# Filter network with summed last weights, and gate products of a recurrence one tile later

## The chip, the cores and the metric

The kernel runs on one core of a Trainium2 chip. The metric is the device time of one execution in microseconds (us), the median of several. A core has TensorE (PE, matmuls), VectorE (DVE), ScalarE (ACT), GpSimd (POOL) and SyncE (SP, which issues loads); each works off its own queue in order, and they wait for each other by semaphores.

## The reference, cut to what matters

Two blocks of two layers each, 512 tokens, 1024 features, float32. The change touches the mixer of the first block, and the filters of the long convolution of the second block, which are computed there in advance.

```python
# block 1, each layer: a gated linear recurrence beside a latent attention
x_rnn, g_rnn, q_lat, kv_lat, k_rope, gate_a, gate_b = split(x @ w_in)
xc = causal_dwconv(x_rnn, conv_w, conv_b)            # 4 taps
gate_x = sigmoid(blockdiag(xc, gx_w) + gx_b)
gate_a_ = sigmoid(blockdiag(xc, ga_w) + ga_b)
log_a = -8 * gate_a_ * softplus(-lambda)
h_t = exp(log_a)_t * h_{t-1} + (sqrt(1 - exp(2 log_a)) * gate_x * xc)_t
y_rnn = gelu(g_rnn) * h
merged = sigmoid(gate_a) * y_rnn + sigmoid(gate_b) * mla_attention(q_lat, kv_lat, k_rope)
# block 2: filters of the long convolution, both layers
hdn = sin(freq2 * (sin(freq1 * (z @ fw1 + fb1)) @ fw2 + fb2))
filt = hdn @ fw3                                     # [512, 512]: forward, backward
h_fwd, h_bwd = filt[:, :256] * window, filt[:, 256:] * window
k = concatenate([h_fwd, 0, h_bwd[:0:-1]])            # backward row 0 is not used
k = k * rsqrt(sum(k * k) + 1e-6);  kf = rfft(k)
```

## The kernel before

Every float32 product is made of three products of float32r parts (`mm3`): high x high, high x low, low x high. So each weight tile is loaded, cast by ScalarE to its high part (`hiw`, line 336), and VectorE subtracts that to get the low part (`low`, line 337). A stream `W` does this in the order in which weights are used: `get(key)` puts the casts and subtractions of all tiles up to two places behind `key` into the queues of ScalarE and VectorE, at this place of the program. Queues keep the order of the program.

Block 1's mixer makes, for each of eight units m (128 features), four tiles of the input product, x, g, a and b: 24 matmuls of 128 x 512 each. `lru(m)` works on them and hands over (`yield`) at five places; at each of these `tick()` takes the next piece of other work, in layer 0 the filter network and its transforms (`filters`), then the rope tables (`rope_tables`, lines 530 to 560), then the rotated key. In layer 1 there are only the latent queries' norm and the rotated key.

The order in `lru(m)` before: the x tile, the convolution (`xc`, on ScalarE and three VectorE instructions), its split into `xch` and `xcl`; tick; the g tile and its gelu; tick; the gate products `za` and `zx` (three matmuls each), their chain s, r, s, thx on ScalarE (Tanh, Exp, Tanh, Tanh) and v2, s_ on VectorE, a Sqrt; tick; the a tile, its tanh `tha`, GpSimd's product v2 * s_ (VectorE's for the first two units of layer 0), VectorE's scan, gl and ysum; tick; the b tile, its tanh `thb`, and 1 added by GpSimd; tick.

Behind the eight units come the attention's values: eight banks (`vb`, six matmuls each), of which ScalarE casts and VectorE subtracts each half in turn (lines 819, 820); then the key's and queries' products and the first scores (line 965).

`filters` computes the hidden layers, then for each of four time tiles t two products with the layers' last weights (line 1189), multiplies each by the window on VectorE, and makes their sum `sp` and difference `sm` by four GpSimd instructions (lines 1193, 1194); sp and sm are split (`hp`, `hm`) at the next tick, the products squared for the norms, and the squares added up by GpSimd (line 1177). The transforms follow, five ticks for each of four tiles of frequencies, with the weights `dft0` in the stream behind g1 to g4.

Of the kernel before, what the change touches and what calls it, by code (L numbers as in the profile page):

```python
# [13 lines left out]
AF = mybir.ActivationFunctionType  # L14
# [3 lines left out]
DEPTH = 2  # L18
S = 512
D = 1024  # L20
P = 128
# [7 lines left out]
# ------------------------------------------------------------------ layout (host, no arithmetic)  # L29
class Cols:  # L30
    """Per-partition vectors side by side in one [128, n] array."""
# [14 lines left out]
def fold(v):  # L46
    """[n*128] -> [128, n]"""
    return np.asarray(v).reshape(-1, P).T


def mtile(w, cols):
    """stationary tile: the columns of w [K, .] as [128, K/128 * len(cols)]"""
    a = w[:, cols]
    k, m = a.shape
    return a.reshape(k // P, P, m).transpose(1, 0, 2).reshape(P, -1)


def lay_out(i):
    """inputs by name -> DRAM arrays, and the places of the vectors"""
# [67 lines left out]
    # constants of the shapes  # L127
# [11 lines left out]
def lay_out2(g, A, V):  # L139
# [38 lines left out]
    # filter network, both layers side by side  # L178
# [19 lines left out]
    # constants of the shapes  # L198
# [9 lines left out]
    wb = wd.copy()  # L208
    wb[0] = 0.0
    A["wind"] = np.concatenate([wd, wb], axis=1).reshape(4, P, 512)  # L210
# [5 lines left out]
    a = np.stack([C, Sn]).reshape(2, 4, P, 4, P)      # part, tt, t, ft, f  # L216
# [25 lines left out]
    for q in range(8):       # token tile q % 4 of the places: token within the tile, tile  # L242
        io[:, 2 * q:2 * q + 2] = np.stack([r + 1, 0 * r + P * (q % 4)], 1)
    io[:, 16:16 + P] = np.arange(P)
    # tokens of an expert above which it may get a second block with the same weights
# [4 lines left out]
# ------------------------------------------------------------------ kernel  # L250
NE = 18         # blocks of 128 tokens: one of every expert, and a second one of the experts in the last two slots
NS = 3          # experts with slots of their own; the others get theirs by the numbers of their tokens
SLOT = list(range(15)) + [14, 15, 15]       # the slot of a block
XH = 5          # places of two halves for loads, during the experts
AHEAD = 5       # slots that are set ahead of the block at work
XRAW = 2        # places for loads beside those of the weights, during the experts
HOFF = 11       # block from which on loads take no further places
LOOP_PLE = {8: 2}       # quarters of the last gates that come between the experts, by their places
# the order of the pieces of an attention step in block 1
ORDER = "ZQqABSNPKTtM"  # L260
# the pieces of work between the steps of the second attention: keys, queries, spectrum and inverse of the
# long convolution, pooling, gate of the convolution
LP = 3          # piece of the output product behind which the second input of the gates is split
NE2 = 9         # step of the second attention in which the norm of the first head ends
# the order within a step: combine, weights, scores, product with the values, transposes, rest, front
WORK = "cwtpsbf"
# weights whose low parts GpSimd takes
# [5 lines left out]
class Stream:  # L273
    """Weights in the order of their use: DMA, then the exact split into two float32r parts."""

    def __init__(self, k, tag, width, raw, bufs, ahead, pool):
        self.pool = pool
        self.k, self.tag, self.width = k, tag, width
        self.nraw, self.bufs, self.ahead = raw, bufs, ahead
        self.items, self.index = [], {}  # L280
        self.dma_at = self.split_at = 0
        self.fence = None         # no loads from there on
        self.stop = None          # no splits from there on
        self.extra = None         # a pool with XRAW more places for loads
        self.halves = 0           # further places, each of two halves
        self.loads = [0, 0, 0, 0]
        self.spots = []           # tiles that are free for loads
        self.raw, self.parts, self.live = {}, {}, 0
        self.lo_engine = lambda n: "gpsimd" if self.items[n][0][0] in ("uq", "uk") else "vector"
# [57 lines left out]
    def fill(self):  # L347
        """loads into every free place"""
# [29 lines left out]
class Kern:  # L378
# [10 lines left out]
    # tiles  # L389
# [21 lines left out]
    # products  # L411
# [6 lines left out]
    def rms_row(self, sq, n, eps):  # L418
        """1 / sqrt(sum over features / n + eps) of every token, as diagonal blocks; sq: squares [features, tokens];
        eps: a number, or one for every token. rms_spread puts them on all partitions"""  # L420
# [28 lines left out]
    # ---- weights in their order  # L449
# [24 lines left out]
    # ---- constants  # L474
# [19 lines left out]
    def lru_constants(self):  # L494
        """4*softplus(-lambda) and its negative, half biases of the gates: for both layers, [128, 16]"""
# [15 lines left out]
        # log1p(e) = 2 atanh(e / (2 + e)), e = exp(-|lambda|) <= 1  # L511
# [10 lines left out]
        # 2 * (2 acc + max(-lambda, 0))  # L522
# [4 lines left out]
    def rope_tables(self):  # L527
# [29 lines left out]
        # the scale of the scores goes into the queries  # L557
# [3 lines left out]
    # ---- layer norm, one tile of 128 tokens at a time  # L561
    def ln_load(self, row, pool):
        """gain and bias rows, on every partition"""
# [7 lines left out]
    def ln_pre(self, t, gb, eps):  # L571
        """t [128, 1024]: normalised in place"""
# [16 lines left out]
    def ln_post(self, t, xt, x):  # L589
        """token tile t of x, transposed and split into xt = (hi, lo) [128, 8, 512]"""  # L590
# [10 lines left out]
    # ---- out[feature, token] tiles  # L601
# [5 lines left out]
    def start_a(self, keys, xt, between):  # L607
        """the first tiles after a layer norm: the first 256 tokens of all, then the others"""
# [12 lines left out]
    # ---- out[token, feature], 1024 features, accumulated in 8 banks  # L621
# [6 lines left out]
    def gemm_b_ln(self, keys, lhs, banks, first, resid, x, xt, gb, eps, tail=4, after=lambda t: None, late=()):  # L628
        """last part of a product with a layer norm behind it; returns what has to come
        between the first tiles of the next product"""  # L630
        n = len(keys)
        if late:
            # the last bank stays free for the pieces of late
# [10 lines left out]
        for t in range(NT):  # L644
# [4 lines left out]
            if t == NT - 1:  # L649
                # the next weights come before the last norm  # L650
# [9 lines left out]
    # ---- block 1  # L660
    def block1_layer(self, l, xt, x_src):
        """xt: the input, transposed and split; x_src: the same in DRAM. Returns x tiles, xt."""
# [3 lines left out]
        # latent queries, keys; norms over features by a product with ones  # L666
# [80 lines left out]
        # gated linear recurrence  # L747
        ysum, thb = [None] * 8, [None] * 8

        def lru(m):  # L750
# [14 lines left out]
            yield  # L765
            zx, za = self.bank("zx"), self.bank("za")
# [12 lines left out]
            # 1 - r^2 = tanh(-log r) (1 + r^2)  # L779
# [4 lines left out]
            yield  # L784
            ab = tile_of(f"a{m}")
            tha = self.k2(name="tha")
            nc.scalar.activation(tha, ab, AF.Tanh, scale=0.5)
# [5 lines left out]
            yield  # L793
            bb = tile_of(f"b{m}")
            thb[m] = self.k2(name="thb")
            nc.scalar.activation(thb[m], bb, AF.Tanh, scale=0.5)
            nc.gpsimd.tensor_scalar(thb[m], thb[m], 1.0, None, op0=OP.add)
# [8 lines left out]
        # latent attention; the values of even and of odd heads, 128 columns for a head: the high part in the half  # L806
        # of its output rows, the low part in the other one
# [25 lines left out]
        # output product, residual, layer norm  # L833
# [15 lines left out]
        # gated convolution feed-forward  # L849
# [59 lines left out]
    def attention(self, l, ap, kvT, qT, kt, vt, ysum, thb, nope_rows):  # L909
        """16 heads; ysum[m] becomes the (hi, lo) of the merged output of head pair m"""  # L910
# [170 lines left out]
    # ------------------------------------------------------------------ block 2  # L1081
    def plan2(self):
        a, W = self.a, self.W
        for l in range(DEPTH):
# [24 lines left out]
            # in the order of the slots' first blocks; the experts of most slots are set when they are known  # L1109
# [11 lines left out]
    def reduce_angle(self, r, arg, m, ki):  # L1121
        """r = arg - 2 pi k, to be wrapped; m, ki are scratch"""
# [20 lines left out]
    def filters(self, fp):  # L1143
        """the convolution filters of both layers: their spectra go to self.kf, the norms to self.hsc"""
# [11 lines left out]
        wind = [load(a["wind"][t], 512, "wn") for t in range(2)]  # L1156
        h = zT
# [16 lines left out]
        def squares():  # L1174
            """the squares of the last tile join those of the first"""
# [3 lines left out]
        for t in range(4):  # L1179
# [5 lines left out]
            sp, sm = self.k2(name="sp"), self.k2(name="sm")  # L1185
            new = []
            for l in range(DEPTH):
                b = self.bank("filt")
                mm(b, lhsT=h[:, P * t:P * t + P], rhs=f3[l], start=True, stop=True)
                f = self.k2(name="filt")  # L1190
                nc.vector.tensor_tensor(f, b, wn, op=OP.mult)
                c = slice(256 * l, 256 * l + 256)
                nc.gpsimd.tensor_tensor(sp[:, c], f[:, :256], f[:, 256:], op=OP.add)
                nc.gpsimd.tensor_tensor(sm[:, c], f[:, 256:], f[:, :256], op=OP.subtract)
                new.append(f)
            squares()
# [11 lines left out]
        for n in range(4):  # L1208
# [37 lines left out]
            if n == 0:  # L1246
                b = self.bank("hsum")
                for l in range(DEPTH):
                    for c in range(2):
                        for s_ in range(2):  # L1250
                            o = 256 * s_ + P * c
                            mm(b[:, 2 * l + c:2 * l + c + 1], lhsT=fs[l][:, o:o + P], rhs=self.ones[:, 0:1],
                               start=s_ == 0, stop=s_ == 1)
                nc.vector.tensor_scalar(self.hsc, b[:, 0:4], 1e-6, None, op0=OP.add)
# [6 lines left out]
    def constants2(self):  # L1261
        """the loads, and what is left to do once they are there"""
# [21 lines left out]
        def rest():  # L1284
# [10 lines left out]
            for l in range(DEPTH):  # L1295
                li = 0.8 - 0.6 * math.exp(-0.3 * l)
                # its negative
# [967 lines left out]
```

## Time and profile before

| what | value |
|---|---|
| device time, median of 3 runs | 2791.44 us (2790.32 to 2793.89) |
| span of the profiled execution | 2785.1 us; the median lies 6.3 us above it |
| TensorE busy | 2646.0 us, 95% |
| VectorE, ScalarE, GpSimd busy | 65%, 50%, 28% |
| units of layer 0, then layer 1 (from x0 to b7) | about 52 to 289 us; 924 to 1111 us |

Busy time counts an engine's instructions from start to end; overlapping ones are counted once. "Idle before" names the engine whose work ended the wait last. The granted clock is TensorE's: 1.00 is 2.4 GHz, 0.5 would be 1.2 GHz.

### The profile page before, as it was taken

The page shows a single profiled execution, that of the slowest core. Times are in us where ns is not written, and L with a number is a line of the kernel's source. Part 1 is how long each engine was busy: PE and PEld are TensorE (multiplying, and loading weights), DVE is VectorE, ACT ScalarE, POOL GpSimd, SP SyncE. Part 2 cuts the span into 40 slices and gives each one's busy share as a digit, 9 for nine tenths or more (in the row PEclk, how much of TensorE's full clock was granted, in tenths as well). Part 3 has the DMA queues.
Part 4 walks back from the last instruction along what each step waited for, and adds up shares of the span by engine and source line. Part 5 has one row for each costly group of instructions (what it writes and reads, how often), then busy time and mean ns, then how long its engine had stood idle before and what let it go on. Part 6 is the DMA issues. An engine that isn't in the chain of part 4 may idle for free. (4 is left out here: it accounts for less than half of the span.)

```text
span 2785.1 us, 36076 instructions
## 1 busy us (share of the span) xinstructions
PE 2646.0 (95%) x13164; PEld 2188.2 (79%) x13164; DVE 1823.3 (65%) x2685; ACT 1394.4 (50%) x2260; POOL 769.4 (28%) x693
## 2 busy tenths in 40 slices
PE   8899999999999999999999997989999989999996
PEld 6687787888888888778888886867877777778875
DVE  6757686663655555686663657577787656777785
ACT  3666773441442566673442431354287625534782
POOL 1411672000001111771000002354343354624332
PEclk9999999999999999999999998999999999999998
DMA  4233113223232232113233232224598742248974
GB/s 159 89 115 109 57 43 115 83 99 113 91 128 99 72 97 90 48 39 136 76 121 106 91 128 97 70 77 161 213 316 281 215 145 81 90 165 276 342 252 146
DMA packets 120527, 364.17 MB, mean 131 GB/s; under 512 B 18900, under 2 KB 24564, under 8 KB 120344
## 3 DMA queue, kind: packets, MB, share of 16 engines
q1 hardware_dynamic: 100088, 320.14, 33.4%
q0 software_dynamic: 20256, 41.67, 5.6%
q8 instruction: 105, 1.72, 0.3%
q14 instruction: 78, 0.64, 0.1%
HBM read 341.80 MB, written 41.94 MB: 138 GB/s over the span
## 5 line engine op out<-in xcount | busy, mean ns | idle before, releaser
L337 DVE TENSOR_TENSOR low<-raww,hiw 128x1024 fp32r<-128x1024 f32 x350 | 439.0, 1266 | 228.9 <-ACT hiw L336 222.2
L336 ACT CAST hiw<-raww 128x1024 fp32r<-128x1024 f32 (+2 forms) x400 | 409.2, 1036 | 216.4 <-PE acc L416 98.7
L582 POOL TENSOR_TENSOR vare<-bnmv,epsc 128x1 f32<-128x1 f32 x36 | 10.1, 281 | 969.6 <-DVE bnmv L579 969.6
L414 PE MATMUL up<-xt,hiw 128*128 128x512 f32 x704 | 273.9, 389 | 0.0
L415 PE MATMUL up<-xt,hiw 128*128 128x512 f32 x704 | 273.9, 389 | 0.0
L416 PE MATMUL up<-xt,low 128*128 128x512 f32 x704 | 273.9, 389 | 0.0
L877 DVE SCALAR_TENSOR_TENSOR cv<-up,vec,cv 128x510 f32<-128x510 f32 (+1 forms) x176 | 131.9, 749 | 144.5 <-ACT cv L874 141.4
L874 ACT ACTIVATE cv<-up,vec 128x512 f32<-128x512 f32 x88 | 68.7, 781 | 234.2 <-PE up L416 234.2
L414 PEld LDWEIGHTS up<-xt,hiw 128*128 128x128 f32 x704 | 132.1, 188 | 27.5
L416 PEld LDWEIGHTS up<-xt,low 128*128 128x128 f32 x704 | 132.1, 188 | 27.4
L415 PEld LDWEIGHTS up<-xt,hiw 128*128 128x128 f32 x704 | 132.1, 188 | 27.3
L414 PE MATMUL acc<-hiw,h2h 128*128 128x512 f32 x384 | 149.6, 389 | 0.0
L416 PE MATMUL acc<-hiw,h2l 128*128 128x512 f32 x384 | 149.4, 389 | 0.0
L415 PE MATMUL acc<-low,h2h 128*128 128x512 f32 x384 | 149.4, 389 | 0.0
L337 POOL TENSOR_TENSOR low<-raww,hiw 128x1024 fp32r<-128x1024 f32 (+1 forms) x50 | 117.6, 2357 | 38.4 <-ACT hiw L336 24.5
L598 ACT CAST xt<-tp 128x512 fp32r<-128x512 f32 x56 | 29.9, 591 | 186.4 <-PE tp L595 186.1
L1766 POOL DMA_INDIRECT yg<-ye,rt x36 | 57.5, 1598 | 226.1 <-ACT ye L1825 198.7
L414 PE MATMUL g<-hiw,xeh 128*128 128x512 f32 x288 | 118.0, 410 | 1.7 <-ACT xeh L446 1.0
L415 PE MATMUL g<-low,xeh 128*128 128x512 f32 x288 | 117.8, 409 | 1.8 <-DVE low L337 1.4
L416 PE MATMUL g<-hiw,xel 128*128 128x512 f32 x288 | 115.0, 399 | 0.0
L990 POOL TENSOR_SCALAR p<-p,lsum 128x128 f32<-128x128 f32 (+2 forms) x96 | 95.6, 1009 | 36.8 <-DVE lsum L986 36.8
L415 PE MATMUL ga<-xt,hiw 128*128 128x256 f32 x320 | 94.7, 296 | 9.5 <-DVE xt L599 9.3
(611 smaller groups left out, 7699.0 us busy)
## 6 DMA issues: line engine op xcount, KB each, us to landing
raww<-in_w_in_dram SPq DMA_DIRECT2D x108, 512.0 KB
raww<-in_w_up_dram SPq DMA_DIRECT2D x96, 512.0 KB
rawh<-in_w_e_dram SPq DMA_DIRECT2D x108, 256.0 KB
raww<-in_w_e_dram SPq DMA_DIRECT2D x50, 512.0 KB
raww<-in_w_down_dram SPq DMA_DIRECT2D x48, 512.0 KB
x<-in_w_e_dram SPq DMA_DIRECT2D x36, 512.0 KB
rawx<-in_w_e_dram SPq DMA_DIRECT2D x32, 512.0 KB
raww<-in_w_out_dram SPq DMA_DIRECT2D x28, 512.0 KB
```

Source lines behind the costliest of these rows:

```text
L336: nc.scalar.copy(hi[:, c], r)
L337: getattr(nc, self.lo_engine(self.split_at)).tensor_tensor(lo[:, c], r, hi[:, c].bitcast(F32), op=OP.subtract)
L414: mm(out, lhsT=lhs[0], rhs=rhs[0], start=start, stop=False)
L415: mm(out, lhsT=lhs[0], rhs=rhs[1], start=False, stop=False)
L416: mm(out, lhsT=lhs[1], rhs=rhs[0], start=False, stop=stop)
L582: nc.gpsimd.tensor_tensor(ve, mv[:, 1:2], self.eps[:, eps:eps + 1], op=OP.add)
L598: nc.scalar.copy(dst[0], src)
L874: nc.scalar.activation(y, b, AF.Identity, bias=self.v(("fb", l), f), scale=self.v(("fw", l, 2), f))
L877: nc.vector.scalar_tensor_tensor(y[:, d:], b[:, :S - d], self.v(("fw", l, k), f), y[:, d:], op0=OP.mult, op1=OP.add)
L990: eng.tensor_scalar(p[:, c], p[:, c], l_[:, i:i + 1], None, op0=OP.mult)
L1766: nc.gpsimd.indirect_dma_start(out=self.yg, out_offset=bass.IndirectOffsetOnAxis(ap=gi[:, e:e + 1] if row is None else row, axis=0), in_=y ...
```

## The change

The last weights of the filter network are summed and subtracted once (`fsd`, four GpSimd instructions); the products with them give sum and difference of the two directions at once, so the sixteen GpSimd instructions of the time tiles fall away. The window's first row is no longer zero for the backward half, so the first row is mended by three instructions on one partition. The squares are those of sum and difference, and are halved. In `lru` the a tile and its tanh come before the gate products, the b tile and its tanh before v2 * s_ and the scan, and there are four ticks instead of five. Comments and the texts of functions fall away too.

```diff
             gl = self.k2(name="gl")
             nc.scalar.activation(gl, gb, AF.Gelu_apprx_tanh)
             yield
+            ab = tile_of(f"a{m}")
+            tha = self.k2(name="tha")
+            nc.scalar.activation(tha, ab, AF.Tanh, scale=0.5)
+            yield
             zx, za = self.bank("zx"), self.bank("za")
...
             nc.vector.scalar_tensor_tensor(v2, thx, 1.0, xc, op0=OP.add, op1=OP.mult)
-            yield
-            ab = tile_of(f"a{m}")
-            tha = self.k2(name="tha")
-            nc.scalar.activation(tha, ab, AF.Tanh, scale=0.5)
+            bb = tile_of(f"b{m}")
+            thb[m] = self.k2(name="thb")
+            nc.scalar.activation(thb[m], bb, AF.Tanh, scale=0.5)
+            nc.gpsimd.tensor_scalar(thb[m], thb[m], 1.0, None, op0=OP.add)
             (nc.vector if l == 0 and m < 2 else nc.gpsimd).tensor_tensor(v2, v2, s_, op=OP.mult)
             nc.vector.tensor_tensor_scan(thx, r, v2, 0.0, op0=OP.mult, op1=OP.add)
             nc.vector.tensor_tensor(gl, gl, thx, op=OP.mult)
             ysum[m] = self.k2(name="ysum")
             nc.vector.scalar_tensor_tensor(ysum[m], tha, 1.0, gl, op0=OP.add, op1=OP.mult)
             yield
-            bb = tile_of(f"b{m}")
-            thb[m] = self.k2(name="thb")
-            nc.scalar.activation(thb[m], bb, AF.Tanh, scale=0.5)
-            nc.gpsimd.tensor_scalar(thb[m], thb[m], 1.0, None, op0=OP.add)
-            yield
...
         wind = [load(a["wind"][t], 512, "wn") for t in range(2)]
+        fsd = [self.k2(name="fsd") for _ in range(2)]
+        for l in range(DEPTH):
+            for y, op in zip(fsd, (OP.add, OP.subtract)):
+                nc.gpsimd.tensor_tensor(y[:, 256 * l:256 * l + 256], f3[l][:, 256:], f3[l][:, :256], op=op)
...
-            sp, sm = self.k2(name="sp"), self.k2(name="sm")
             new = []
-            for l in range(DEPTH):
+            for w in fsd:
                 b = self.bank("filt")
-                mm(b, lhsT=h[:, P * t:P * t + P], rhs=f3[l], start=True, stop=True)
+                mm(b, lhsT=h[:, P * t:P * t + P], rhs=w, start=True, stop=True)
                 f = self.k2(name="filt")
                 nc.vector.tensor_tensor(f, b, wn, op=OP.mult)
-                c = slice(256 * l, 256 * l + 256)
-                nc.gpsimd.tensor_tensor(sp[:, c], f[:, :256], f[:, 256:], op=OP.add)
-                nc.gpsimd.tensor_tensor(sm[:, c], f[:, 256:], f[:, :256], op=OP.subtract)
                 new.append(f)
+            sp, sm = new
+            if t == 0:
+                nc.vector.tensor_tensor(sm[0:1], sm[0:1], sp[0:1], op=OP.subtract)
+                nc.vector.tensor_scalar(sm[0:1], sm[0:1], 0.5, None, op0=OP.mult)
+                nc.vector.tensor_scalar(sp[0:1], sm[0:1], -1.0, None, op0=OP.mult)
             squares()
...
-                nc.vector.tensor_scalar(self.hsc, b[:, 0:4], 1e-6, None, op0=OP.add)
+                nc.vector.tensor_scalar(self.hsc, b[:, 0:4], 0.5, 1e-6, op0=OP.mult, op1=OP.add)
```

## Rows read from the trace of the kernel before

**Rows 1.** The page: span, and busy time of the engines (share) xinstructions.

```profile
span 2785.1 us, 36076 instructions
...
PE 2646.0 (95%) x13164; PEld 2188.2 (79%) x13164; DVE 1823.3 (65%) x2685; ACT 1394.4 (50%) x2260; POOL 769.4 (28%) x693
```

**Rows 2.** TensorE's waits, 70 to 115 us: total, times, longest.

```profile
PE za L414 <- ACT xch L446: 5.5, 1, 5.5
...
PE in_g L416 <- DVE low L337: 1.7, 1, 1.7
...
PE za L415 <- DVE xcl L447: 0.7, 1, 0.7
```

**Rows 3.** Windows of early layer 0: length, busy by engine, granted clock, DMA.

```profile
66.00:104.60 38.60, 30.93 (x120) 21.77 (x118) 29.35 (x38) 24.33 (x35) 21.54 (x22) 0.99 0.24 75
...
104.60:114.00 9.40, 8.71 (x27) 6.66 (x28) 8.17 (x7) 9.31 (x14) 5.68 (x4) 0.69 0.15 43
```

**Rows 4.** TensorE's waits, 215 to 262 us, and 900 to 1130 us.

```profile
PE in_g L416 <- DVE low L337: 2.2, 1, 2.2
...
PE in_x L416 <- DVE low L337: 0.8, 1, 0.8
```

**Rows 5.** ScalarE's timeline, layer 1, unit 6: start, duration, instruction [idle before].

```profile
1073.92 0.62 ACT L446 CAST xch<-xc 128x512 fp32r<-128x512 f32 x1 [2.44 <-DVE xc L756]
...
1077.61 0.69 ACT L772 ACTIVATE s<-za,hba 128x512 f32<-128x512 f32 x1
...
1086.05 0.60 ACT L787 ACTIVATE tha<-in_a 128x512 f32<-128x512 f32 x1
...
1086.54 1.04 ACT L336 CAST hiw<-raww 128x1024 fp32r<-128x1024 f32 x1
...
1088.38 0.60 ACT L796 ACTIVATE thb<-in_b 128x512 f32<-128x512 f32 x1 [0.80 <-PE in_b L416]
```

**Rows 6.** ScalarE's timeline, layer 1, end of unit 7 and values.

```profile
1111.50 0.60 ACT L796 ACTIVATE thb<-in_b 128x512 f32<-128x512 f32 x1 [1.12 <-PE in_b L416]
...
1116.00 0.88 ACT L819 CAST v<-vb 128x256 fp32r<-128x256 f32 x2 [0.49 <-DVE v L820]
```

**Rows 7.** VectorE's timeline, layer 0, 90 to 97 us.

```profile
90.00 0.68 DVE L447 TENSOR_TENSOR hp<-sp,hp 128x512 fp32r<-128x512 f32 x1
...
95.75 1.81 DVE L447 TENSOR_TENSOR hp<-sp,hp 128x512 fp32r<-128x512 f32 x1 [1.97 <-ACT hp L446]
```

**Rows 8.** TensorE's timeline, layer 0, about 66 us.

```profile
66.00 1.88 PE L1189 MATMUL filt<-f,rad 128*128 128x512 f32 x4
...
67.31 0.79 PE L414 MATMUL za<-xch,hig 128*128 128x512 f32 x1
```

**Rows 9.** GpSimd's timeline, layer 0 at 216 us, layer 1 at 1107 us.

```profile
215.91 1.49 POOL L797 TENSOR_SCALAR thb<-thb 128x512 f32<-128x512 f32 x1 [4.34 <-ACT thb L796]
...
1106.73 1.29 POOL L788 TENSOR_TENSOR v<-v,s 128x512 f32<-128x512 f32 x1 [15.33 <-ACT s L782]
```

**Rows 10.** VectorE's timeline, layer 1, units 6 and 7 and values.

```profile
1071.52 2.32 DVE L756 SCALAR_TENSOR_TENSOR xc<-in_x,vec,xc 128x509 f32<-128x509 f32 x3 [3.02 <-ACT xc L753]
...
1109.03 1.21 DVE L789 TENSOR_TENSOR_SCAN thx<-r,v 128x512 f32<-128x512 f32 x1
...
1111.68 1.22 DVE L337 TENSOR_TENSOR low<-raww,hiw 128x1024 fp32r<-128x1024 f32 x1
...
1114.14 0.42 DVE L820 TENSOR_TENSOR v<-vb,v 128x256 fp32r<-128x256 f32 x1 [1.24 <-ACT v L819]
```

**Rows 11.** Rope tables in layer 0: timelines of ScalarE and of VectorE.

```profile
235.83 1.28 ACT L542 ACT_TABLE_LOAD   x1
...
237.12 0.63 ACT L542 ACTIVATE Sg<-ang 128x512 f32<-128x512 f32 x1
...
253.62 0.42 DVE L552 COPY TE<-C 32x512 f32<-32x512 f32 x1
```

**Rows 12.** TensorE's timeline, first scores of layer 1.

```profile
1130.56 0.38 PE L965 MATMUL s<-k,qh 128*128 128x256 f32 x1 [1.79 <-ACT qh L446]
```

More of the change, by code (lines that the diff above doesn't have):

```diff
@@ L207, in lay_out2 @@
     wd = np.exp(-t * np.abs(de)).astype(f4)
-    wb = wd.copy()
-    wb[0] = 0.0
-    A["wind"] = np.concatenate([wd, wb], axis=1).reshape(4, P, 512)
+    A["wind"] = np.concatenate([wd, wd], axis=1).reshape(4, P, 512)
     tt, ff = np.arange(S, dtype=np.float64), np.arange(S, dtype=np.float64)
@@ L1250, in filters @@
                         for s_ in range(2):
-                            o = 256 * s_ + P * c
-                            mm(b[:, 2 * l + c:2 * l + c + 1], lhsT=fs[l][:, o:o + P], rhs=self.ones[:, 0:1],
+                            o = 256 * l + P * c
+                            mm(b[:, 2 * l + c:2 * l + c + 1], lhsT=fs[s_][:, o:o + P], rhs=self.ones[:, 0:1],
                                start=s_ == 0, stop=s_ == 1)
-                nc.vector.tensor_scalar(self.hsc, b[:, 0:4], 1e-6, None, op0=OP.add)
+                nc.vector.tensor_scalar(self.hsc, b[:, 0:4], 0.5, 1e-6, op0=OP.mult, op1=OP.add)
                 nc.gpsimd.tensor_tensor(self.hsc, self.hsc, self.eps[:, 2:3].to_broadcast([P, 4]), op=OP.pow)
```

## The prediction

> **What bounds the kernel now.** I read the page first: TensorE is busy 95% of a 2785.1 us span [rows 1], so a change pays only where TensorE stands idle or is made to. The edited code works in two stretches, the mixers of block 1's two layers (about 52 to 300 us and 929 to 1124 us). Then I read who TensorE waited for there. Layer 0, early: three waits of 5.5, 1.7 and 0.7 us [rows 2], behind which the granted clock is 0.69 for 9.4 us [rows 3]. Layer 0, late: one of 2.2 us beside the rope tables [rows 4]. In layer 1 nothing above 0.8 us [rows 4]. So some 13 us can be won at most: 7.9 of early waits, 9.4 x 0.31 = 2.9 of clock, 2.2 late. Last I laid the queues of the other engines beside each other, since each works in program order: what is queued behind a waiting instruction decides.
>
> **The period.** The tanh on the b tile recurs after 1111.50 - 1088.38 = 23.12 us [rows 5, 6]: four tiles of 24 matmuls and six gate matmuls, so 0.227 us each, 5.44 a tile, 1.36 for the gates. TensorE does the same products afterwards; only order changes.
>
> **Part 1, filter network.** Of four time tiles each loses four GpSimd instructions of 256 columns (16), and four such additions come once, with the network's loads, six tiles of TensorE's work ahead of the first filter product at 66.0 us [rows 8], the first to wait for them. They cost nothing; at most their length, four halves of a 1.29 us instruction [rows 9], 2.6 us. VectorE's two multiplications a tile stay; three one-row instructions come for the first tile, each no longer than a full-width one of 0.68 [rows 7]: below 2.1, I take 1.7. The conversions no longer wait for GpSimd, but the squares now overwrite the sum and difference, so ScalarE must wait until VectorE has read them: a new hand-off of some 0.9 us a tile.
>
> What that is worth is read early in layer 0. From 66.0 to 104.6 us VectorE is busy 29.35 us and ScalarE 24.33 [rows 3]: TensorE waits there because the two hand work to each other late, and because VectorE's conversions take 1.81 us beside GpSimd instead of 0.68 [rows 7]. Afterwards TensorE asks next for the second a tile: its products before it are a0, b0, x1, g1 (21.8), z0 (1.36), four filter products (1.31 each, from 66.00 to 67.31 [rows 8]) and four changes from them back to the tiles (the first matmul behind takes 0.79 for 0.39, so 0.4 each): 30 us after 66, at 96. Its low weights stand in VectorE's queue behind all that rows 3 count (29.35, less 2.2 for the conversions that GpSimd slowed, two of them by 1.13) and behind 4 us more (a convolution's conversion 0.7, gate weights 0.4, the one-row work 1.7, itself 1.2): ready 31 us after 66 without any wait, so 1 to 2 us late. With ScalarE's own turns between (its weights' cast comes behind the squares of the third tile, which wait for VectorE) I lay it out at 103 to 104, some 7.5 late, with the same slow clock behind it. So the early stall moves from the gates of unit 1 to its a tile: 7.9 before, 7.5 after. I take a gain of 0.5; the ends are -2 (the squares' hand-off costs more) and +9 (1.5 late, no fall of the clock: 10.8 - 1.5).
>
> The Trainium skill, "GPSIMD Engine Reference", section 1 Specifications, says that GpSimd's SBUF interfaces are shared with VectorE, with contention for instructions with two SBUF inputs. The slowed conversions are such instructions. By that rule with 12 GpSimd instructions fewer the early gain would lie near the +9; it is a rival below.
>
> **Part 2, the ticks.** A unit has four places for filter work instead of five, so the transforms and the rope tables come later: the latter in units 6 and 7 instead of 5 to 6. In units 2 to 5 TensorE has up to 5.5 us of transform products a unit more than 23.12, which covers ScalarE's and VectorE's copies: no cost. The 2.2 us wait [rows 4] goes; I leave 0.4 for unit 7's b weights behind the rope's wrap: gain 1.8. In layer 1 the small waits at its first unit (about 1) go as well, since the next x weights are split before the gates' chain: gain 1, with 0 to 1 lost again below.
>
> **Part 3, the gates a tile later: what is late next.** This is the sum's main term. Before, the a tile (5.44) and the b tile (5.44) both run behind the gates; their chain ended under the b tile. Afterwards only b does, and one order is new: GpSimd's multiplication v2*s stands behind thb + 1, which waits for b's tanh; VectorE's scan waits for that multiplication. The loop, from ScalarE's s of one unit to the next:
> - s to the tanh behind Sqrt, one weights' cast and two table loads between: 1086.05 - 1077.61 = 8.44 [rows 5], now on b;
> - that tanh 0.60 [rows 5], GpSimd 1.49 and 1.29 [rows 9];
> - scan to the next weights' low part: 1111.68 - 1109.03 = 2.65; that part 1.22 [rows 10];
> - convolution to the cast of its result: 1073.92 - 1071.52 = 2.40 [rows 5, 10];
> - cast to s: 3.69, and now a weights' cast and the a tanh ahead of s: 1.04 + 0.49 [rows 5].
>
> Sum 23.31, against TensorE's 23.12. In layer 1 that is a tie: 0.2 x 7 units at most, first eaten by about 1 us of slack. In layer 0 it is covered by the transforms. So inside the loop I take 0 to 1 us, and set it against the 1 us of part 2.
>
> At the end of unit 7 nothing covers it. Behind it come the attention's values: per bank ScalarE casts and VectorE subtracts, by turns. Before, b ended at about 1111.3 (its tanh began at 1111.50 on TensorE's release [rows 6]) and VectorE's first subtraction stood at 1114.14 [rows 10]: 2.8 us later. After: the first gate product za ends 5.44 + 0.68 = 6.1 before b's end; s follows 0.2 later, at -5.9; then 8.44 + 0.60 + 1.49 + 1.29 + 2.65 = 14.47: VectorE is free at +8.6. That is 5.8 us later than before. In layer 1 the first unit's latent norms and rope leave ScalarE some 0.7 behind, so 6.5. In layer 0 unit 7 also carries the rest of the rope: a Sin with its table load (1.28 + 0.63 [rows 11]) and another load ahead of the a tanh (1.28), so s comes 3.2 later, and the rope's last VectorE instructions, which began at 253.62 in unit 6 before [rows 11], stand ahead of v2, by my layout for another 0.3: 9.3.
>
> Can this be made good? The values' turn goes 0.88 + 0.49 = 1.37 us a bank [rows 6], and the six matmuls of a bank take 6 x 0.227 = 1.36: no catching up. Behind the eight banks the first scores wait for the query's split even now (1.8 us [rows 12]), so TensorE there follows ScalarE and VectorE, and a delay passes to it whole. So the tail costs 6.5 + 9.3 = 15.8; the ends are 11.6 (twice 5.8, no lag, no rope) and 20 (GpSimd's add slowed and 2 us of lag in each layer).
>
> **Sum.** +15.8 (tail) - 0.5 (early) - 1.8 (late wait) - 1 + 0.5 (layer 1) = +13; the early term's ends lie unevenly, more gain than loss, so I round to +12. The profiled execution's span is 2785.1, and the median of its runs 2791.44, 6.3 more, which stays. Forecast 2803.
>
> **Rivals.**
> - *The early stall goes* (ends on the other side: not slower). Place: unit 1's a weights in layer 0. Without GpSimd beside it VectorE has them ready 1 to 2 us late, and the clock doesn't fall. For it: the slowed conversions [rows 7]; against it: ScalarE's turns, and that even without waits it is late. Gain 9 instead of 0.5: +12 - 8.5 = +3.5, 2795, which is no change. It decides if the tail costs under 17.
> - *The tail is not paid*: the values' subtractions get in ahead of the scan, or the queries' chain has slack that I don't see. For it: TensorE has eight banks to fill, 10.9 us of work, and the key and query products behind them; against it: the turn of 1.37 us and the wait on the query [rows 6, 12]. Then +12 - 15.8 = about -4, 2787, down to 2779 with the early gain.
> - *The loop is longer than the tile period*: the thb + 1 takes some 0.8 us more than 1.49 when VectorE works beside it. Then each of seven units of layer 1 loses 0.8 to 1 once the slack is gone: +5, 2808.
>
> **How the numbers follow.** About 0.2% (5.6 us) is what a measurement here can tell from no change. Chances: forecast, +6 to +16, 0.52; longer loop, +16 to +21, 0.12; early stall gone, +1 to +5.5, 0.16; tail not paid, -12 to +2, 0.20, of which 0.12 lies beyond -5.6. So faster 0.12, same 0.24, slower 0.64. The range 2786 to 2812 leaves out half of the tail's rival below and the end of the loop's above. The forecast's own range is 2797 to 2807.
>
> **What would show it.** In the profile after: TensorE waiting in layer 0 for the weights of in_a, not of za, between 95 and 106 us; no wait for in_g near 230; VectorE's first v subtraction 8 to 10 us behind b's last matmul in layer 1 and about 12 in layer 0, and a longer wait for the first scores; GpSimd's v2*s directly behind thb + 1; no more than 1 us of waits inside layer 1's units. I am wrong if the first scores follow b7 as closely as before (then I misread the values' turn), or if TensorE runs through 96 to 104 us (then I overrated the hand-offs).

## The result, and the profile after

The changed kernel takes 2808.28 us (median of 4 runs, 2807.71 to 2810.01); the kernel before, beside it, 2790.88 (4 runs). The ratio is 1.0068 [1.0056, 1.008]: 19 us slower, where 12 were forecast (the two medians lie 17.4 apart). That is above the forecast's own range of +6 to +16; it lies in the band that the prediction gave to its rival of the longer loop. The page of the profiled execution has a span 21.2 us longer than that of [rows 1], with the same 13164 matmuls and 12 GpSimd instructions fewer:

```profile
span 2806.3 us, 36056 instructions
...
PE 2650.4 (94%) x13164; PEld 2193.6 (78%) x13164; DVE 1822.9 (65%) x2688; ACT 1393.3 (50%) x2260; POOL 754.4 (27%) x681
```

**The early stall.** TensorE's waits between 60 and 130 us (total, times, longest), then two windows of that stretch (columns as in [rows 3]):

```profile
PE in_a L412 <- ACT hiw L334: 8.6, 1, 8.6
PE in_b L412 <- ACT gl L762: 1.4, 1, 1.4
PE in_a L414 <- DVE low L335: 1.0, 1, 1.0
```

```profile
66.00:104.60 38.60, 29.38 (x116) 21.26 (x114) 29.61 (x43) 26.26 (x39) 6.11 (x5) 0.94 0.24 80
104.60:114.00 9.40, 7.60 (x18) 5.53 (x19) 7.08 (x6) 6.79 (x9) 4.41 (x4) 0.54 0.19 58
```

The wait stands at unit 1's a tile now, not at za [rows 2]. GpSimd is busy for 6.11 us of the first window instead of 21.54 [rows 3], yet VectorE is as busy as before, 29.61 to 29.35, and the wait did not get shorter. The second window's clock is 0.54, where it was 0.69.

**The tails.** What follows the last b tile is where the time went. TensorE's waits from 280 to 335 us and from 1100 to 1165, then the first scores of both layers in its timeline:

```profile
PE s L962 <- ACT qh L444: 7.8, 1, 7.8
PE vb L412 <- ACT hiw L334: 4.1, 1, 4.1
...
PE s L962 <- ACT qh L444: 7.5, 1, 7.5
PE vb L412 <- ACT hiw L334: 1.1, 1, 1.1
```

```profile
319.59 0.58 PE L962 MATMUL s<-k,qh 128*128 128x256 f32 x1 [7.85 <-ACT qh L444]
...
1151.30 0.58 PE L962 MATMUL s<-k,qh 128*128 128x256 f32 x1 [7.46 <-ACT qh L444]
```

In the kernel before, layer 1's first scores stand at 1130.56 [rows 12]; layer 0's, and its first VectorE subtraction of the values, in the timelines of TensorE and VectorE:

```profile
308.01 0.39 PE L965 MATMUL s<-k,qh 128*128 128x256 f32 x1 [1.73 <-ACT qh L446]
...
291.65 0.42 DVE L820 TENSOR_TENSOR v<-vb,v 128x256 fp32r<-128x256 f32 x1 [1.22 <-ACT v L819]
```

I measure a tail from the start of unit 7's last b matmul to the start of the first scores. In layer 0 that is 288.35 to 308.01 before and 288.14 to 319.59 after, 19.66 and 31.45; in layer 1 1111.08 to 1130.56 and 1122.98 to 1151.30, 19.48 and 28.32. So the tails grew by 11.8 and 8.8, 20.6 us in all, of a span that grew by 21.2. Up to the end of layer 0's b tile the two kernels differ by 0.2 us, and from layer 0's first scores to layer 1's last b matmul they take 803.07 and 803.39. So nearly all of the growth is in the tails.

That last pair hides two differences that cancel. Layer 1's units, from their first matmul (before, then after) to the last b matmul, take 187.40 us before and 185.75 after:

```profile
923.68 0.48 PE L414 MATMUL in_x<-xt,hiw 128*128 128x512 f32 x1
...
937.23 0.48 PE L412 MATMUL in_x<-xt,hiw 128*128 128x512 f32 x1
```

So the new order gains 1.65 us there; the waits of 0.8 and 0.3 us in layer 1's first unit are gone. The stretch ahead of them, from layer 0's first scores on, is 2.0 longer, 617.64 against 615.67: in the 20 us behind these scores the granted clock is 1.00 before and 0.87 after.

How layer 1's tail is made is seen by laying three engines beside each other, VectorE, GpSimd and ScalarE:

```profile
1129.88 3.39 DVE L791 TENSOR_TENSOR_SCAN thx<-r,v 128x512 f32<-128x512 f32 x1 [3.50 <-POOL v L790]
1133.31 2.15 DVE L792 TENSOR_TENSOR gl<-gl,thx 128x512 f32<-128x512 f32 x1
1135.49 0.69 DVE L794 SCALAR_TENSOR_TENSOR ysum<-tha,gl 128x512 f32<-128x512 f32 x1
1136.10 0.42 DVE L817 TENSOR_TENSOR v<-vb,v 128x256 fp32r<-128x256 f32 x1
```

```profile
1127.11 1.49 POOL L789 TENSOR_SCALAR thb<-thb 128x512 f32<-128x512 f32 x1 [20.14 <-ACT thb L788]
1128.57 1.27 POOL L790 TENSOR_TENSOR v<-v,s 128x512 f32<-128x512 f32 x1
1129.80 5.11 POOL L335 TENSOR_TENSOR low<-raww,hiw 128x1024 fp32r<-128x1024 f32 x2
...
1132.15 2.76 POOL L335 TENSOR_TENSOR low<-raww,hiw 128x768 fp32r<-128x768 f32 x1
```

```profile
1126.43 0.60 ACT L788 ACTIVATE thb<-in_b 128x512 f32<-128x512 f32 x1
...
1136.55 0.65 ACT L816 CAST v<-vb 128x256 fp32r<-128x256 f32 x2 [7.58 <-DVE v L817]
```

The scan waits 3.50 us for v2*s, which stands behind thb + 1. That was forecast. Not forecast: the scan then takes 3.39 instead of 1.21 and the product with the gelu 2.15 instead of 0.69. GpSimd has gone on to its low parts of the attention's weights (the last line is the second of the two), and the engines take turns. The first low part ends about 1132.2, and the scan 1.1 later; the second, begun at 1132.15, ends 1.6 behind the scan; the product ends 0.6 behind that. Layer 0 shows the same on VectorE:

```profile
298.10 3.40 DVE L791 TENSOR_TENSOR_SCAN thx<-r,v 128x512 f32<-128x512 f32 x1 [3.57 <-POOL v L790]
301.52 2.15 DVE L792 TENSOR_TENSOR gl<-gl,thx 128x512 f32<-128x512 f32 x1
...
304.39 0.42 DVE L817 TENSOR_TENSOR v<-vb,v 128x256 fp32r<-128x256 f32 x1
```

### The profile page after: what moved, and what is told of

It is laid out like the page before. It is cut to its first block, busy times and chain, and to the rows that moved or that the text cites. A ratio compares the mean times of both kernels' runs of the same rounds, so it can differ in the third digit from the quotient of the medians.

```text
span 2806.3 us, 36056 instructions
## 1 busy us (share of the span) xinstructions
PE 2650.4 (94%) x13164; PEld 2193.6 (78%) x13164; DVE 1822.9 (65%) x2688; ACT 1393.3 (50%) x2260; POOL 754.4 (27%) x681
## 5 line engine op out<-in xcount | busy, mean ns | idle before, releaser
L335 DVE TENSOR_TENSOR low<-raww,hiw 128x1024 fp32r<-128x1024 f32 x350 | 433.1, 1248 | 243.0 <-ACT hiw L334 242.3
L789 POOL TENSOR_SCALAR thb<-thb 128x512 f32<-128x512 f32 x16 | 25.7, 1609 | 302.2 <-ACT thb L788 302.2
```

The source lines that it names most:

```text
L335: getattr(nc, self.lo_engine(self.split_at)).tensor_tensor(lo[:, c], r, hi[:, c].bitcast(F32), op=OP.subtract)
```

## The experiments

The theory (A): the order on GpSimd's queue behind the last b tile, and GpSimd's low parts beside VectorE there, make the whole difference; the filter network and the units' loop make none. The rivals: each unit loses a little; the filter network costs the time; the slow scan has another cause. All runs in one table (ratio to the kernel before; for the profiled execution the start of layer 0's last b matmul and the two tails, us):

| kernel | ratio | last b, layer 0 | tail, layer 0 | tail, layer 1 |
|---|---|---|---|---|
| before | 1 | 288.35 | 19.66 | 19.48 |
| after | 1.0068 [1.0056, 1.008] | 288.14 | 31.45 | 28.32 |
| filters alone | 0.9993 [0.9984, 1.0002] | 289.09 | 19.70 | 19.45 |
| order alone | 1.0052 [1.0033, 1.0072] | 284.74 | 31.42 | 28.27 |
| two lines exchanged | 1.0017 [1.0008, 1.0026] | 284.95 | 24.80 | 20.99 |
| last unit in the old order | 1.0055 [1.0042, 1.0068] | 290.88 | 30.46 | 18.69 |
| GpSimd's low parts held | 1.0034 [1.0021, 1.0047] | 286.48 | 27.79 | 24.64 |
| exchanged, fifth places | 0.9997 [0.9985, 1.0008] | 285.94 | 22.27 | 20.98 |
| mixed | 0.9986 [0.9976, 0.9997] | 285.54 | 22.31 | 19.45 |
| mixed, old filters | 0.9988 [0.9979, 0.9997] | 282.87 | 22.30 | 19.44 |
| mixed, filters spread | 1.0012 [1.0002, 1.0023] | 291.60 | 22.29 | 19.45 |
| exchanged, squares apart | 1.0013 [1.0002, 1.0023] | 285.33 | 23.43 | 22.31 |

**Filters alone** (the new filter network, `lru` as before).

> The filter network of the changed kernel with the recurrence's order of before (part 1 alone). Theory A: part 1 is worth little either way: no tail is added, the first scores follow the last b tile as in the kernel before, and the early waits of layer 0 (7.9 us before) change by -2 to +2 with the same slow clock behind them: 2787 to 2793. Rival B (the filter network itself costs the time, through its longer hand-off between VectorE and ScalarE): 2797 or more. Rival D (the early waits go for want of GpSimd beside VectorE): 2780 to 2784.

Measured: 0.9993, not to be told from no change, and the tails are those of before. The early waits keep their place and a similar size; these are TensorE's waits from 60 to 130 us, which add up to 6.8, against 8.4 before (the largest of each kernel's early waits stays at za):

```profile
PE za L412 <- ACT xch L444: 3.1, 1, 3.1
PE in_g L414 <- DVE low L335: 1.5, 1, 1.5
```

Theory A stands, the rivals B and D fall.

**Order alone** (the new `lru`, the filter network as before).

> The recurrence's order of the changed kernel with the filter network of before (parts 2 and 3 alone). Theory A (part 1 alone measured 0.9993; the parts add up): 1.0068 / 0.9993 = 1.0075, so 19 to 23 us over the kernel before, with the same tails in both layers. Rival (part 1 pays only in the new order, where the a tile stands at the stall: its four GpSimd instructions a tile are then in the way): the early wait of 8.6 grows, 25 us or more over the kernel before.

Measured: 1.0052, with the tails of the changed kernel to 0.1 us, and 7.4 for the wait at unit 1's a tile. That is some 14 us, less than the 19 to 23 expected, but the interval holds 1.0068. The order alone makes the loss, and no part of it is shown to come from the filter network.

**Two lines exchanged** in the changed kernel:

```diff
-            nc.gpsimd.tensor_scalar(thb[m], thb[m], 1.0, None, op0=OP.add)
             (nc.vector if l == 0 and m < 2 else nc.gpsimd).tensor_tensor(v2, v2, s_, op=OP.mult)
+            nc.gpsimd.tensor_scalar(thb[m], thb[m], 1.0, None, op0=OP.add)
```

> The changed kernel with two lines exchanged: GpSimd multiplies v2*s before it adds 1 to the tanh of the b tile, not behind it. Theory A (the tail is made by order on GpSimd): in the last unit v2*s starts when Sqrt is done (about 1124.2 instead of 1128.57 in layer 1, 292.5 instead of 296.79 in layer 0), the scan only waits for VectorE's low part ahead of it (about 1126.4 and 294.5 instead of 1129.88 and 298.10), and it takes 1.2 again, as GpSimd's low parts begin behind it. VectorE's first subtraction of the values comes 7 us earlier in each layer; 0.7 a layer is lost again as the low parts now stand beside the values' turns. Sum -13: 2795, at most -16. Rival B (the time went into the unit loop or the filter network, and the tail only shows it): the exchange leaves the time at 2806 to 2809. Rival C (what counts is only that b's tanh is later than before; the order on GpSimd is hidden by VectorE's queue): the scan moves by under 2 us and the time falls by 4 at most.

Measured: 1.0017, 0.0051 or 14 us less; the tails are shorter by 6.7 and 7.3. Layer 1's GpSimd and VectorE, in the stretch that answers to the one shown above:

```profile
1113.87 1.27 POOL L789 TENSOR_TENSOR v<-v,s 128x512 f32<-128x512 f32 x1 [18.39 <-ACT s L784]
1116.67 1.98 POOL L790 TENSOR_SCALAR thb<-thb 128x512 f32<-128x512 f32 x1 [1.52 <-ACT thb L788]
1118.62 4.49 POOL L335 TENSOR_TENSOR low<-raww,hiw 128x1024 fp32r<-128x1024 f32 x2
```

```profile
1116.15 1.21 DVE L791 TENSOR_TENSOR_SCAN thx<-r,v 128x512 f32<-128x512 f32 x1
1117.40 0.92 DVE L792 TENSOR_TENSOR gl<-gl,thx 128x512 f32<-128x512 f32 x1
...
1118.96 0.42 DVE L817 TENSOR_TENSOR v<-vb,v 128x256 fp32r<-128x256 f32 x1
```

v2*s is done before b's tanh has come, the scan waits for nothing and takes 1.21, and the low parts begin at 1118.62, as ysum ends. Theory A stands; B and C fall. Of the 19 us, 14 hung on the order of two lines.

**GpSimd's low parts held**: the changed kernel, and ahead of the attention

```diff
         run_all(fgen)
         fx.close()
+        hold = self.small(4, "hold")
+        nc.gpsimd.tensor_copy(hold[:, 0:1], ysum[7][:, 0:1])
```

> The changed kernel with one GpSimd copy of a single column of the last unit's ysum ahead of its low parts for the attention's weights, so that these begin only when the scan, the product with the gelu and ysum are done. Theory A2 (the two low parts make VectorE's scan take 3.40 instead of 1.22 and the product 2.15 instead of 0.69): both are at 1.2 and 0.7 again, VectorE's first subtraction comes 3.6 us earlier in each layer, of which 0.7 is lost since the low parts then slow the values' turns: -5 to -7, 2801 to 2803. Rival (the scan is long because of its own operands or the PSUM traffic then, not GpSimd's low parts): it stays at 3.4, and the time at 2808 or a little above.

Measured: 1.0034, 9 us less than the changed kernel where 5 to 7 were expected; the tails are shorter by 3.66 and 3.68. VectorE and GpSimd in layer 1:

```profile
1126.82 1.22 DVE L791 TENSOR_TENSOR_SCAN thx<-r,v 128x512 f32<-128x512 f32 x1 [3.51 <-POOL v L790]
1128.08 0.69 DVE L792 TENSOR_TENSOR gl<-gl,thx 128x512 f32<-128x512 f32 x1
...
1129.42 0.42 DVE L819 TENSOR_TENSOR v<-vb,v 128x256 fp32r<-128x256 f32 x1
```

```profile
1129.57 0.18 POOL L803 COPY hold<-ysum 128x1 f32<-128x1 f32 x1 [2.78 <-DVE ysum L794]
1129.71 4.21 POOL L335 TENSOR_TENSOR low<-raww,hiw 128x1024 fp32r<-128x1024 f32 x2
```

The wait for v2*s is the same 3.5 us; the scan and the product have their old lengths. So the slowness was GpSimd's low parts, and it was worth 3.7 us a layer. The 0.7 that I expected to lose again did not come: beside the values' subtractions, which read PSUM, the low parts take 4.21, and neither is slowed.

**The last unit in the old order**: in the changed kernel unit 7 alone has gates, a tile, b tile (`tile_a` and `tile_b` hold the lines of these tiles).

```diff
+            if m < 7:
+                tha = tile_a()
+                yield
             zx, za = self.bank("zx"), self.bank("za")
...
-            bb = tile_of(f"b{m}")
+            if m < 7:
+                tile_b()
+            else:
+                yield
+                tha = tile_a()
...
+            if m == 7:
+                tile_b()
             yield
```

> The changed kernel with only the last unit of each layer in the order of before (gates, then its a tile, then its b tile); units 0 to 6 stay in the new order. Theory A: the loss sits behind the last unit alone. Layer 1's first scores come 8 to 9 us earlier, layer 0's 8 to 12 (the rope tables still end in the last unit there, which may keep some 3 us): -16 to -20, 2788 to 2792. Rival B (loss spread over the units, 1 us in each): only an eighth is won back, -2 to -3, 2805.

Measured: 1.0055, only 4 us less: the forecast of this run was wrong in both theories' terms. Layer 1's tail is short, 18.69, as A has it; but new waits take the gain away. TensorE's waits from 1100 to 1165 us and from 280 to 335:

```profile
PE za L412 <- ACT xch L444: 2.6, 1, 2.6
...
PE vb L413 <- DVE low L335: 9.7, 2, 6.5
```

With no a tile between, unit 7's gates come 5.4 us earlier and wait for the convolution, which stands behind unit 6's late scan (2.6 us in layer 1, 2.2 in layer 0). In layer 0 the rope still ends in unit 7, so VectorE's scan comes late there, beside GpSimd's low parts, and the values' last weights' low part stands behind it:

```profile
294.48 3.38 DVE L802 TENSOR_TENSOR_SCAN thx<-r,v 128x512 f32<-128x512 f32 x1
...
300.84 1.21 DVE L335 TENSOR_TENSOR low<-raww,hiw 128x1024 fp32r<-128x1024 f32 x1
```

**Exchanged, fifth places.** With the exchange layer 0's tail is still 5.1 us over that of before, layer 1's only 1.5.

```diff
+            if l == 0 and 2 <= m < 7:
+                yield
             bb = tile_of(f"b{m}")
```

> The kernel with the two GpSimd lines exchanged, and with a fifth place for filter work in units 2 to 6 of layer 0, so that the rope tables end before the last unit, as in the kernel before. Theory A (layer 0's tail, which in the exchanged kernel is still 24.80 us from the end of the last b tile to the first scores, where layer 1 has 20.99, is longer by the rope that stands in its last unit): it falls to 21 to 22, -3 to -4 us: ratio to the kernel before 1.0004 (0.999 to 1.001). Rival (rope hidden; it is the weights' casts that are late): 24 to 25, ratio 1.0017 as without.

Measured: 0.9997, layer 0's tail 22.27; first scores at 308.21, as before:

```profile
308.21 0.39 PE L964 MATMUL s<-k,qh 128*128 128x256 f32 x1 [1.78 <-ACT qh L444]
```

So four places instead of five were part of the loss. The rope's own share is less than the 2.5 us between 24.80 and 22.27. The waits for the values' weights (`vb`) fall by 1.4 us in all, from 1.7 and 1.2 to 0.5 and 1.1. The rest can be the clock: the kernel of the last experiment below has the code of the exchanged one in this tail and the same two waits, yet its tail is 23.43; the granted clock from 293 to 297 us is 1.00 there and 0.71 in the exchanged kernel.

**Mixed**: the same in layer 0, and layer 1 wholly in the old order (gates, a, b, each behind a place of its own).

> As the kernel with the exchange and the fifth places in layer 0, and with layer 1 wholly in the order of before. Theory A (layer 1 gains nothing from the new order, since TensorE waits for nothing inside its units in either, and pays 1.5 us in the tail even with the exchange: 20.99 against 19.48): 1.5 us less than with the fifth places alone, ratio 0.9998 (0.9985 to 1.0005). Rival (the new order saves some 1 us within layer 1): same or slower than with the fifth places alone.

Measured: 0.9986 [0.9976, 0.9997], 4 us faster than the kernel before, and layer 1's tail is back to 19.45. But layer 1 as a whole gained nothing by this: its units take 187.41 us again, against 185.76 with the fifth places alone, and units and tail together 206.86 against 206.74. So the premise of theory A is wrong, and layer 1 does what the rival says. Of all kernels in the table this is the lowest ratio. New in it are a last b matmul 2.8 us earlier in layer 0 and a tail 2.7 longer there, so the profiled execution shows no gain (span 2785.3); the gain rests on the timed runs, and where it comes from stays open.

**Mixed, old filters**, and **mixed, filters spread** (an empty place behind each time tile from the second on, and one place fewer behind each of the first three tiles of frequencies; the diff is that of the spread kernel).

```diff
             squares()
             yield
+            if t:
+                yield
...
                 yield
                 yield
-                yield
```

> As the mixed kernel (layer 0 in the new order with the two GpSimd lines exchanged and the fifth places, layer 1 in the old order), with the filter network of before. Theory A (in the new order the changed filter network costs time, where it was worth 0.0007 in the old one: its two-column sums of squares on GpSimd stand beside VectorE's weight low part, which takes 2.13 where it takes 1.46 beside the old network's narrower additions): the wait for unit 1's a weights is 7.4 as in the kernel with the old network and the new order, 3 to 5 us less in all: ratio 0.997 (0.996 to 0.998). Rival (the difference of 0.0016 between these two was spread of the runs): ratio 0.9986 to 0.9993.

> As the mixed kernel, with the filter network's four time tiles at every other place from the second on (three more empty places there, one fewer behind each of the first three transforms). Theory A (the early wait of 8.6 us in layer 0 comes of VectorE's queue: from 66 to 105 us it works 30 of 39 us, and each tile puts its two low parts, two multiplications and two sums of GpSimd beside them, 2.6 us and a slowed low part of 1 us more, ahead of the a weights): one of the tiles moves out from in front and the wait falls to 3 to 6, nothing new in the units behind: -3 to -6 us with the clock, ratio 0.9970. Rival (the wait moves on to the tiles of unit 1 or 2 that follow): sum of the early waits within 2 us of 9.6, ratio 0.9986.

Measured: 0.9988 with the old filters, where the mixed kernel has 0.9986. That is the rival: the wait at unit 1's a tile is 7.4 instead of 8.6, and the time does not show it. Part 1 is worth nothing that can be measured in either order. With the filters spread: 1.0012, 7 us more than the mixed kernel. The rival was right that the wait moves on, but more was lost than it says: the early waits add up to 12.1, not to 9.6 within 2. TensorE's waits from 60 to 130 and from 130 to 225 us, and the window behind (TensorE first, the clock third from the end):

```profile
PE in_a L412 <- ACT hiw L334: 6.2, 1, 6.2
PE in_a L414 <- DVE low L335: 0.9, 1, 0.9
...
PE in_a L412 <- ACT hiw L334: 3.5, 1, 3.5
PE in_a L414 <- DVE low L335: 1.5, 1, 1.5
```

```profile
130.00:150.00 20.00, 15.05 (x54) 11.73 (x53) 8.21 (x11) 9.70 (x16) 3.08 (x3) 0.83 0.26 86
```

2.5 us were won in unit 1 and 5.0 lost in unit 2, with a second stretch of lower clock (0.83, where the mixed kernel has 1.00).

**Exchanged, squares apart**: the squares get buffers of their own.

```diff
             for f in new:
-                nc.scalar.activation(f, f, AF.Square)
-            fs += new
+                q = self.k2(name="filt2")
+                nc.scalar.activation(q, f, AF.Square)
+                fs.append(q)
```

> The kernel with the two GpSimd lines exchanged, with the filters' squares written to buffers of their own instead of over the sum and the difference, so that ScalarE's squares no longer wait until VectorE has made the low parts from these. Theory A (the wait of 8.6 us for unit 1's a weights in layer 0 is made of these hand-offs: the squares wait 2.50 us at 94.25, the weights' cast, VectorE's low part and the convolution come behind them, and so does GpSimd's sum of the squares, beside which that low part takes 2.13 instead of 1.22): the wait falls by 1.5 to 3.5, to 5 to 7, and 1 us more comes back as the clock falls for a shorter time: -2 to -4 us, ratio 1.0007. Rival (VectorE's queue alone makes it late): the wait stays above 8, ratio 1.0017.

Measured: 1.0013 against 1.0017, and the wait is 8.5. The squares wait for nothing now (the weights' cast behind them starts at 91.69 instead of 95.39), but their sums on GpSimd come earlier too and meet VectorE's next low part. GpSimd's line comes first, then VectorE's, then ScalarE's cast of the convolution's result, behind which the a weights' cast stands:

```profile
92.80 2.53 POOL L1179 TENSOR_TENSOR filt<-filt,filt 128x512 f32<-128x512 f32 x2
...
92.52 3.37 DVE L445 TENSOR_TENSOR hp<-filt,hp 128x512 fp32r<-128x512 f32 x1
...
101.14 0.62 ACT L444 CAST xch<-xc 128x512 fp32r<-128x512 f32 x1 [7.73 <-DVE xc L754]
```

3.37 for 0.69: a hand-off of 2.5 us was turned into a collision of 2.7. The forecast of theory A fails, but the run doesn't separate the two theories, since one delay took the other's place. What the lines show is that ScalarE stood 7.73 us waiting for VectorE's convolution, which came at the end of VectorE's queue.

## Why the prediction came out as it did

**The tail's mechanism was right, its size 4.8 us short.** The step that failed is the sum "8.44 + 0.60 + 1.49 + 1.29 + 2.65": the 2.65 from scan to free VectorE was taken from a stretch in which GpSimd was idle [rows 10]: its v2 * s_ ended at 1108.0 [rows 9], and its next instruction began at 1112.19. The edit puts GpSimd's low parts, next in its queue, right beside the scan. With 3.39 and 2.15 for 1.21 and 0.69 VectorE is free 3.6 later in each layer; holding the low parts back gave 3.7 a layer. Against that, "no catching up" was wrong by 1.2 a layer: the 1.37 of a bank [rows 6] was TensorE's own pace, and after a long wait the banks stand full, so the turn takes 1.195 ((1143.72 - 1136.55) / 6, from ScalarE's casts). First subtraction to last: 10.4 before, 9.2 after, in both layers. Layer 1: 6.5 + 3.6 - 1.2 = 8.9, measured 8.8. Layer 0: 9.3 + 3.6 - 1.2 = 11.7, measured 11.8. In the traces VectorE's first subtraction stands 13.1 us (layer 1) and 16.3 us (layer 0) behind the start of the last b matmul, where 8 to 10 and about 12 were forecast. The end of 20 named a slowed add, not a slowed scan.

The Trainium skill, "SBUF — State Buffer", section "SBUF: two separate sides", says that VectorE and GpSimd share one pair of SBUF ports as an exclusive lock, held for a whole instruction, against VectorE instructions with two SBUF inputs. The traces agree for GpSimd's low parts, which have two inputs: scan and product end about one undisturbed length (1.21, 0.69) after a low part, and subtractions with an input in PSUM are not slowed. They don't agree for thb + 1, which has one: in the exchanged kernel the product with the gelu began and ended while it ran, 0.92 instead of 0.69, so nothing was locked out for a whole instruction. The prediction weighed the milder sentence of another page against the filters alone, and not against the tail.

**The early stall** went from za to unit 1's a tile as forecast, but with 8.6 + 1.0 instead of 7.5, and a granted clock behind it of 0.54 instead of 0.69, so the gain of 0.5 did not come. The reason given, VectorE's queue, fits the traces, but no run shows it alone: taking GpSimd's sixteen instructions away (filters alone) left the time as it was, and without the hand-offs (squares apart) a collision took their place. Of the rival, that the stall goes, nothing came.

**The late wait** went (2.2 before, 0.3 after at unit 7's b tile). **Of the forecast gain of 2.3 in layer 0 only 0.2 arrived.** There the a and b tiles of later units waited 1.1 us in all (0.5, 0.3, 0.3), which the text had covered by the transforms; the exchange removes these waits, and its last b matmul stands 3.2 earlier. So the order on GpSimd cost something inside layer 0's loop as well. The other part of that difference isn't settled: the wait of 1.4 for in_b comes in some executions of the same early code and not in others (not in the held kernel, and against that one the exchange's last b matmul is 1.5 earlier). **In layer 1 the gain came**, 1.65 instead of 0.5, since the loop lost nothing there. With the order alone, the low parts held or the squares apart the units take 187.35 all the same; there the granted clock of their first 4 us is 0.57 instead of 1.00. The 2.0 us of lower clock behind layer 0's first scores, which the sum did not have, took the gain away. The rival of the longer loop did not happen. So it is partly luck that the time lies inside 2786 to 2812: the forecast's own range ends at 2807, and what lies above it was there for that rival.

**The sum**: +13 before it was rounded to +12; with the tail's two corrections (+7.2 - 2.4) +17.8; without the 2.1 that didn't come in layer 0 +19.9; with the 2.0 of lower clock and layer 1's further 1.15 of gain +20.75; 0.5 more lies behind layer 1's first scores. That is the 21.2 of the profiled span. The ratio gives +19.

## What to carry to other kernels

When an instruction is moved on a queue, cost not only its wait but what the freed engine does next, and beside whom: over a third of the price here (7.3 of 19 us) was GpSimd going on to work that blocked VectorE on the path; the exchange of the two lines removes this too. In a hand-written order put the producer that somebody waits for ahead of the one that nobody waits for; here two lines made 14 us, these 7.3 among them. A loop whose work is covered says nothing about its last turn: lay that one out by itself, with what follows it.

## What the runs showed of the hardware

A VectorE instruction with both inputs in SBUF stood still while GpSimd's two-input instruction ran, 3.39 us for a scan of 1.21 and up to 3.37 for a subtraction of 0.69, and the other way round (a low part 2.76 beside the scan; the two low parts 5.11 against 4.21). With one input in PSUM neither was slowed (0.42 and 4.21 in the held kernel). Beside thb + 1, which reads one input, the product with the gelu took 0.92 for 0.69 in the exchanged kernel, so that case cost far less here.

The clock after a short wait differed between executions: in the tail the values waited 0.5 and 1.1 us for their weights both in layer 1 of the kernel with the fifth places and in layer 0 of the mixed kernel, but the granted clock of the 4 us behind was 1.00 there (the upper level, 2.4 GHz) and 0.57 here, near the lower one (1.2 GHz is 0.50); the tails differ by 1.3 us (20.98 and 22.31).
